# Instructions that read freshly loaded decay rows, queued behind the latest traced eviction

## The chip, the cores and the metric

The kernel runs on one core of one Trainium2 chip. The time is that of one execution on the device in microseconds (us); a run is repeated and the median is given. TensorE (PE in the profile) multiplies into PSUM, VectorE (DVE), ScalarE (ACT) and GpSimd (POOL) work elementwise, and SyncE (SP) issues transfers. Each engine takes its instructions in the order of its own queue, and an instruction that waits holds up those behind it.

## What is computed

One layer of a streaming encoder over 576 frames (a prompt of 512 and a sample of 64) of width 1024, in float32:

```python
def layer(x, lp, st):
    h = x + 0.5 * swiglu(rmsnorm(x, lp['norm_ffn1']), lp['w_ffn1_in'], lp['w_ffn1_out'])
    mix, new_st = mixer(rmsnorm(h, lp['norm_mix']), lp, st)
    h = h + mix
    h = h + 0.5 * swiglu(rmsnorm(h, lp['norm_ffn2']), lp['w_ffn2_in'], lp['w_ffn2_out'])
    return h, new_st
```

The mixer projects its input once and feeds three branches: band attention of 8 heads, an SSD scan (Mamba-2) of 16 heads in 4 groups, and an mLSTM scan of 4 heads. Both scans weigh products of a chunk with decays, exponentials of differences of running sums. For the SSD scan:

```python
cum = jnp.cumsum(dtc * a, axis=1)
seg = cum[:, :, None] - cum[:, None, :]
lmat = jnp.exp(jnp.where(causal, seg, -jnp.inf))
cb = jnp.einsum('btgn,bsgn->btsg', cc, bc)
w = cb[..., None] * lmat * dtc[:, None]
y = jnp.einsum('btsgr,bsgrp->btgrp', w, xc)
y = y + jnp.exp(cum)[..., None] * jnp.einsum('btgn,bgrpn->btgrp', cc, h)
last = cum[:, -1]
wd = jnp.exp(last[:, None] - cum) * dtc
h = jnp.exp(last)[..., None, None] * h + jnp.einsum('bsgr,bsgn,bsgrp->bgrpn', wd, bc, xc)
```

The mLSTM scan has the same shape, with a running maximum as stabiliser.

## The kernel before

Activations lie with features on the 128 partitions and the 576 frames along the free axis. A float32 product is made of three products of rounded parts (high by high, high by low, low by high): ACT rounds a weight piece (line 334) and DVE takes the rest (line 335). Most products go through seven block products in place of eight on 2x2 blocks of the matrices: POOL and accumulating transfers add the weight blocks (lines 548 and 560), and each product (line 704, twelve matmuls) lands in a PSUM bank.

In the mixer the projections are a stream of such products, seven to a pair of output tiles (`pairs`). Each product's bank is emptied by one instruction: `tmp` (line 621, ACT, into `uv`), or `emit` (line 628 on ACT, line 630 on DVE). The evictions have a raised priority. The next product but a few in the same bank can start only when its bank has been emptied.

Between the products the branches' own work is traced as jobs. `product` calls `tick`, which lets the job at the head of a list trace its next piece, up to a `yield n` that asks for n ticks of pause. The jobs are attention (`attn`), mLSTM heads (`ml`) and SSD groups (`ssd`), in the order a0 a1 m0 s0 a2 a3 s1 m1 s2 m2 s3 m3.

The decay rows are computed once (`gates`), written to DRAM (`scr`) and loaded back spread over the partitions: `decays` loads a pair of rows (line 188, ACT's queue) into one of three pairs of slots of `R1` (R in the profile), one pair ahead of its use; `ssd` also loads a pair into `ec` (line 1359, ACT's queue). What reads them:

- `ml`: `qt` = q times a row (line 1158, POOL); D from the row and a column of the small table TM (line 1162, DVE, five pieces), then Exp; `wc` (line 1180, ACT, five columns).
- `ssd`, for each of two halves of a group: `wd` (lines 1333 and 1334, DVE), `el` (1336 and 1337, ACT), Exp of `wd` (1338), which scales x into `xw` (1342, ACT); Relu of each of two rows in five pieces (1349, ACT), then Exp (1351 and 1352), then POOL's product with cb (1353 and 1354), which TensorE multiplies (1392); and Exp of `ec` (1383, ACT). TensorE uses `xw` for the states (1367). Each group starts with six Silu instructions (1287 and 1290).

The order on each engine is a planner's: it runs through the traced instructions with its own estimate of times and takes, on each engine, what is ready, the earliest traced first but for raised priorities. An instruction can thus stand on its engine far ahead of others that were traced before it, if its inputs are ready by that estimate. `issue_after(i)` adds an order of issue behind `i` for what a block traces on `i`'s engine, with no wait for its end; `keep_in_program_order(i)` puts `i` behind the instruction traced last ahead of it on its engine.

Of the kernel before, what the change touches and what calls it, by code (L numbers as in the profile page):

```python
# [28 lines left out]
AF = mybir.ActivationFunctionType  # L29
ALU = mybir.AluOpType  # L30
# [5 lines left out]
CH = [(0, 128), (128, 128), (256, 128), (384, 128), (512, 64)]  # L36
# [49 lines left out]
class Hybrid:  # L86
    def __init__(self, ctx, tc, I, O):
        self.tc, self.nc, self.I, self.O = tc, tc.nc, I, O
        self.op = None
        self.stay = {}  # L90
        self.plan = []
        self.splan = []
        self.ahead = {}
        self.steps = None
        self.b_i, self.b_n, self.fetched = 0, 0, deque()
        self.behind = 0
        self.jobs, self.gap, self.side = deque(), 0, iter(())
# [12 lines left out]
        self.gs = [self.dram.tile([128, T], F32, name=f"gs{i}") for i in range(24)]  # L110
        self.scr = self.dram.tile([24, T], F32, name="scr_rows")
# [496 lines left out]
    def pairs(self, seq):  # L608

        nc = self.nc
        order = ((0, self.T_X1), (0, self.T_A11), (1, self.T_A22), (0, self.T_X4), (0, self.T_X3), (1, self.T_X2),
                 (0, self.T_A21))
        H = (slice(0, FH), slice(FH, T))

        def tmp(ps, scale):
            o = self.gp.tile([128, FH], F32, name="uv", tag="uv", bufs=4)
            with self.tc.high_priority(offset=EVAC):  # L620
                nc.scalar.activation(o, ps, AF.Copy, scale=scale)  # L621
            return o

        def emit(ps, scale, other=None, op=None):
            def go(dst, a=0, b=FH, func=None):
                with self.tc.high_priority(offset=EVAC):
                    if other is None:
                        nc.scalar.activation(dst, ps[:, a:b], func or AF.Copy, scale=scale)  # L628
                        return
                    nc.vector.scalar_tensor_tensor(dst, ps[:, a:b], scale, other[:, a:b], op0=ALU.mult, op1=op)  # L630
                if func:
                    nc.scalar.activation(dst, dst, func)
            return go

        def pair(tiles, done):
            ((name, c1), s1, put1), ((_, c2), s2, put2) = tiles
            o = {}

            def on(t, ps):
                if t == self.T_X1:  # L640
                    o["v"] = tmp(ps, s1)
                elif t == self.T_X4:
                    o["m6"] = tmp(ps, s2)
                elif t == self.T_A11:
                    put1(1, H[1], emit(ps, s1, o["v"], ALU.add))
                elif t == self.T_X3:
                    o["u"] = tmp(ps, s2)
                elif t == self.T_A21:
                    put2(1, H[1], emit(ps, s2, o["u"], ALU.subtract))
                elif t == self.T_A22:  # L650
                    put2(0, H[0], emit(ps, -s2, o["m6"], ALU.add))
                else:
                    put1(0, H[0], emit(ps, s1))
                    if done:
                        done()
            return (name, 0, c1, c2), self.T, on

        self.stream([pair(*p) for p in seq], order, lambda n: {self.T_X1: n % 2, self.T_X4: 2, self.T_A11: 2})

    def tick(self):
        next(self.side, None)
# [479 lines left out]
    def ml(self, h, t):  # L1144
        nc = self.nc
        q, k, v, o = t["q"], t["k"], t["v"], t["o"]
        i = self.b()
        nmB, eiB = self.R1[:, i, :], self.R1[:, i + 1, :]
# [6 lines left out]
        self.tok_major(v, v1)  # L1155
        yield 1
        qt = self.t("t")
        nc.gpsimd.tensor_tensor(qt, q, eiB, op=ALU.mult)

        D = self.P()  # L1160
        for c, (a, n) in enumerate(CH):
            nc.vector.tensor_scalar(D[:n, a:a + n], nmB[:n, a:a + n], self.TM[:n, c, 64 + h:65 + h], 0.0,
                                    op0=ALU.add, op1=ALU.min)
        nc.scalar.activation(D[:, :512], D[:, :512], AF.Exp)
        nc.scalar.activation(D[:64, 512:], D[:64, 512:], AF.Exp)
        dv = D[:, :512].rearrange("p (c t) -> p c t", t=128)
# [2 lines left out]
        s = self.ps("s")  # L1169
# [6 lines left out]
        self.empties(nc.vector.tensor_tensor(D[:64, 512:], s2[:64, :64], D[:64, 512:], op=ALU.mult))  # L1176

        wc = self.unit([128, 8], "wc", 2)
        for c, (a, n) in enumerate(CH):
            nc.scalar.activation(wc[:n, c:c + 1], self.TM[:n, c, 64 + h:65 + h], AF.Exp, bias=nmB[:n, a + n - 1:a + n])  # L1180
        yield 2
        nums = [self.ps("v"), self.ps("x")]
        where = [(0, 0), (0, 129), (0, 258), (1, 0), (1, 129)]
# [1 line left out]
        for c, (a, n) in enumerate(CH):  # L1185
# [22 lines left out]
        r = self.unit([128, 8], "r", 2)  # L1208
# [3 lines left out]
        for c, (a, n) in enumerate(CH):  # L1212
            b, o0 = where[c]
# [3 lines left out]
        for c, (a, n) in enumerate(CH):  # L1217
            b, o0 = where[c]
# [63 lines left out]
    def ssd(self, g, t):  # L1282
        nc = self.nc
# [3 lines left out]
        last = nc.scalar.activation(self.R1[:, 0, :], self.R1[:, 0, :], AF.Silu)  # L1287
# [8 lines left out]
        ps = self.ps("s")  # L1296
# [5 lines left out]
        ps = self.ps("s")  # L1302
# [6 lines left out]
        for j in range(2):  # L1309
            x = t[f"x{j}"]  # L1310
            d0 = 4 * g + 2 * j
            i = self.b()
            free += [i, i + 1]
            cum = self.R1[:, i, :], self.R1[:, i + 1, :]
# [4 lines left out]
            ps = self.ps("x")  # L1319
# [4 lines left out]
            ps = self.ps("x")  # L1324
# [3 lines left out]
            wd = self.unit([128, 5, 2], "wd", 2)  # L1328
            el = self.unit([128, 5, 2], "el", 2)
            nc.gpsimd.memset(wd[:, 4, :], 0.0)  # L1330
            for r in range(2):
                last = cum[r][:, 127:512:128]
                nc.vector.tensor_tensor(wd[:, 0:4, r], last, self.TM[:, 0:4, 32 + d0 + r], op=ALU.subtract)
                nc.vector.tensor_tensor(wd[:64, 4:5, r], cum[r][:64, 575:576], self.TM[:64, 4:5, 32 + d0 + r],
                                        op=ALU.subtract)
                nc.scalar.activation(el[:, 0:4, r], last, AF.Exp)
                nc.scalar.activation(el[:, 4:5, r], cum[r][:, 575:576], AF.Exp)
            nc.scalar.activation(wd, wd, AF.Exp)
            for c, (a, n) in enumerate(CH):
                for r in range(2):  # L1340
                    hs = slice(r * 64, (r + 1) * 64)
# [3 lines left out]
            for r in range(2):  # L1345
                e = cum[r]
                tc_ = 32 + d0 + r
                for c, (a, n) in enumerate(CH):
                    nc.scalar.activation(e[:n, a:a + n], e[:n, a:a + n], AF.Relu, scale=-1.0,
                                         bias=self.TM[:n, c, tc_:tc_ + 1])  # L1350
                nc.scalar.activation(e[:, :512], e[:, :512], AF.Exp, scale=-1.0)
                nc.scalar.activation(e[:64, 512:], e[:64, 512:], AF.Exp, scale=-1.0)
# [10 lines left out]
            for c, (a, n) in enumerate(CH):  # L1363
                if c == 4:
                    states[4] = s0
                ps = self.ps("s")
                nc.tensor.matmul(ps[:, :128], bt[:n, c, :], xw[:n, c, :], start=True, stop=True)
                new = st()
                if c == 0:
                    i = nc.scalar.copy(new, ps[:, :128])  # L1370
                else:
                    h = states[c]
                    for r in range(2):
                        hs = slice(r * 64, (r + 1) * 64)
                        i = nc.vector.scalar_tensor_tensor(new[:, hs], h[:, hs], el[:, c, r:r + 1], ps[:, hs],
                                                           op0=ALU.mult, op1=ALU.add)
# [6 lines left out]
            nc.scalar.activation(ec, ec, AF.Exp)  # L1383
# [368 lines left out]
```

## Time and profile before

| | |
|---|---|
| median of 3 runs | 1923.6 us (1921.49 to 1924.52) |
| profiled execution | 1917.74 us |
| its span, first to last instruction | 1916.0 us |
| mean granted TensorE clock | 0.992 |
| transfers of rows into R (line 188) | 12 of 576 KB, median 5.8 us to landing |
| transfers into `ec` (line 1359) | 16 of 144 KB, median 5.4 us to landing |

The profile is of one execution. Busy time is the time in which an engine ran at least one instruction; TensorE's is modelled, as its matmuls are pipelined. Where a row ends in brackets, they hold how long the engine stood idle before that instruction and what it waited for last. A granted clock of 1.00 is TensorE's full speed.

### The profile page before, as it was taken

The page shows a single profiled execution, that of the slowest core. Times are in us where ns is not written, and L with a number is a line of the kernel's source. Part 1 is how long each engine was busy: PE and PEld are TensorE (multiplying, and loading weights), DVE is VectorE, ACT ScalarE, POOL GpSimd, SP SyncE. Part 2 cuts the span into 40 slices and gives each one's busy share as a digit, 9 for nine tenths or more (in the row PEclk, how much of TensorE's full clock was granted, in tenths as well). Part 3 has the DMA queues.
Part 4 walks back from the last instruction along what each step waited for, and adds up shares of the span by engine and source line. Part 5 has one row for each costly group of instructions (what it writes and reads, how often), then busy time and mean ns, then how long its engine had stood idle before and what let it go on. Part 6 is the DMA issues. An engine that isn't in the chain of part 4 may idle for free. (4 is left out here: it accounts for less than half of the span.)

```text
span 1916.0 us, 37655 instructions
## 1 busy us (share of the span) xinstructions
PE 1862.7 (97%) x13901; PEld 1811.8 (95%) x13901; DVE 1534.0 (80%) x2715; ACT 1090.5 (57%) x2502; POOL 673.1 (35%) x645
## 2 busy tenths in 40 slices
PE   9899999999999989999999999999999999999998
PEld 9899999999999769988989889999999999999998
DVE  7998998998768858678787866745898998889865
ACT  6564654654534786777766666334565564554544
POOL 3433333343302225324445343530334333333311
PEclk9999999999999999999999999999999999999999
DMA  7366666666643445764667665642546666666631
GB/s 224 103 154 173 162 156 165 154 176 170 176 133 99 139 140 142 211 174 116 178 165 186 169 159 168 215 171 80 124 111 168 169 154 169 165 155 168 154 99 56
DMA packets 129439, 294.69 MB, mean 154 GB/s; under 512 B 14288, under 2 KB 26192, under 8 KB 129256
## 3 DMA queue, kind: packets, MB, share of 16 engines
q1 hardware_dynamic: 99368, 203.42, 32.6%
q0 software_dynamic: 20272, 74.20, 21.0%
q10 hardware_dynamic: 9616, 14.69, 2.7%
q8 instruction: 109, 1.79, 0.4%
q14 instruction: 74, 0.61, 0.1%
HBM read 272.87 MB, written 19.38 MB: 153 GB/s over the span
## 5 line engine op out<-in xcount | busy, mean ns | idle before, releaser
L704 PE MATMUL acc<-TH,ph 128*128 128x288 f32 x3220 | 965.0, 300 | 28.3 <-ACT uv L621 9.0
L704 PE MATMUL acc<-TL,ph 128*128 128x288 f32 x3220 | 954.7, 297 | 1.3 <-DVE TL L335 1.2
L704 PE MATMUL acc<-TH,pl 128*128 128x288 f32 x3220 | 950.6, 296 | 0.3 <-DVE pl L335 0.3
L704 PEld LDWEIGHTS acc<-TH,ph 128*128 128x128 f32 x3220 | 605.8, 188 | 46.7 <-ACT uv L621 12.2
L704 PEld LDWEIGHTS acc<-TL,ph 128*128 128x128 f32 x3220 | 607.3, 189 | 3.8 <-DVE TL L335 2.4
L704 PEld LDWEIGHTS acc<-TH,pl 128*128 128x128 f32 x3220 | 607.6, 189 | 3.0 <-issue 2.1
L335 DVE TENSOR_TENSOR pl<-wr,ph 128x512 fp32r<-128x512 f32 x471 | 443.7, 948 | 72.9 <-ACT ph L334 61.2
L334 ACT CAST ph<-wr 128x512 fp32r<-128x512 f32 x471 | 287.5, 618 | 262.1 <-PE acc L704 136.6
L335 DVE TENSOR_TENSOR pl<-wx,ph 128x512 fp32r<-128x512 f32 x390 | 325.9, 839 | 35.1 <-ACT ph L334 28.8
L334 ACT CAST ph<-wx 128x512 fp32r<-128x512 f32 x390 | 237.0, 619 | 183.8 <-POOL wx L560 98.8
L560 POOL TENSOR_TENSOR wx<-wx,wr 128x512 f32<-128x512 f32 x160 | 246.3, 1540 | 184.9 <-DVE pl L335 150.2
L548 POOL DMA_DIRECT2D wx<-in_sblk x115 | 101.5, 916 | 482.5 <-DVE pl L335 167.6
L279 PE MATMUL acc<-YH,ph 128*128 128x256 f32 (+1 forms) x768 | 227.1, 298 | 2.4 <-ACT g L628 2.0
L279 PE MATMUL acc<-YL,ph 128*128 128x256 f32 (+1 forms) x768 | 227.2, 297 | 0.6 <-DVE YL L392 0.6
L279 PE MATMUL acc<-YH,pl 128*128 128x256 f32 (+1 forms) x768 | 226.9, 296 | 0.0
L279 PEld LDWEIGHTS acc<-YH,ph 128*128 128x128 f32 x768 | 145.2, 190 | 3.4 <-ACT g L628 2.2
L279 PEld LDWEIGHTS acc<-YL,ph 128*128 128x128 f32 x768 | 145.3, 189 | 1.1 <-DVE YL L392 1.0
L279 PEld LDWEIGHTS acc<-YH,pl 128*128 128x128 f32 x768 | 145.2, 189 | 0.0
L560 POOL TENSOR_TENSOR wy<-wx,wr 128x512 f32<-128x512 f32 x35 | 55.7, 1591 | 128.3 <-DVE pl L335 90.2
L743 DVE SCALAR_TENSOR_TENSOR R<-acc,R 128x288 f32<-128x288 f32 x168 | 75.7, 451 | 19.3 <-PE acc L704 18.8
L334 ACT CAST TH<-g 128x288 fp32r<-128x288 f32 x120 | 51.4, 433 | 53.4 <-POOL g L729 32.3
L335 DVE TENSOR_TENSOR pl<-wy,ph 128x512 fp32r<-128x512 f32 x70 | 62.0, 886 | 19.7 <-ACT ph L334 19.5
(330 smaller groups left out, 2351.7 us busy)
## 6 DMA issues: line engine op xcount, KB each, us to landing
wr<-in_sblk SPq DMA_DIRECT2D x345, 256.0 KB, 3.8
wx<-in_sblk POOLq DMA_DIRECT2D x119, 512.0 KB, 6.7
wx<-in_sblk SPq DMA_DIRECT2D x111, 512.0 KB, 3.8
wr<-in_wblk SPq DMA_DIRECT2D x126, 256.0 KB, 3.1
R<-scr_rows ACTq DMA_DIRECT2D x12, 576.0 KB, 5.8
gs<-g SPq DMA_DIRECT2D x20, 288.0 KB, 2.9
g<-gs POOLq DMA_DIRECT2D x20, 288.0 KB, 3.8
y<-ys POOLq DMA_DIRECT2D x12, 288.0 KB, 4.8
```

The costliest lines, as they stand in the source:

```text
L279: last = nc.tensor.matmul(ps[:, :n], wt[:, wsl], xx[:, k0 + k, a:a + n], start=(k == 0 and i == 0), stop=(k == nk - 1 and i == 2))
L334: self.cast = self.nc.scalar.copy(hi, src).ins
L335: self.nc.vector.tensor_tensor(lo, src, hi.bitcast(F32), op=ALU.subtract)
L548: nc.gpsimd.dma_start(x12, src[:, 1:3, :], accum_op=ALU.add)
L560: add = lambda o, one, two: self.nc.gpsimd.tensor_tensor(o, one, two, op=ALU.add)
L704: self.nc.tensor.matmul(ps, wt[:, wsl], xx[:, kk, :], start=(start and kk == 0 and i == 0), stop=(kk == 3 and i == 2), skip_group_check=True)
L743: self.nc.vector.scalar_tensor_tensor(o, ps, scale, o, op0=ALU.mult, op1=ALU.add)
```

## The change

The kernel remembers the last traced eviction on ACT and on DVE. A block `behind_products` queues what is traced in it on either engine behind that engine's remembered eviction. The instructions that read freshly loaded rows on ACT and DVE are put in such blocks, and `qt` on POOL is kept behind the instruction traced ahead of it.

```diff
+        self.evicted = {}
...
-                nc.scalar.activation(o, ps, AF.Copy, scale=scale)
+                self.evicted["ACT"] = nc.scalar.activation(o, ps, AF.Copy, scale=scale).ins
...
-                        nc.scalar.activation(dst, ps[:, a:b], func or AF.Copy, scale=scale)
+                        self.evicted["ACT"] = nc.scalar.activation(dst, ps[:, a:b], func or AF.Copy, scale=scale).ins
                         return
-                    nc.vector.scalar_tensor_tensor(dst, ps[:, a:b], scale, other[:, a:b], op0=ALU.mult, op1=op)
+                    self.evicted["DVE"] = nc.vector.scalar_tensor_tensor(dst, ps[:, a:b], scale, other[:, a:b],
+                                                                         op0=ALU.mult, op1=op).ins
...
+    @contextmanager
+    def behind_products(self):
+
+        with ExitStack() as s:
+            for i in self.evicted.values():
+                s.enter_context(self.tc.issue_after(i))
+            yield
...
-        nc.gpsimd.tensor_tensor(qt, q, eiB, op=ALU.mult)
+        self.tc.keep_in_program_order(nc.gpsimd.tensor_tensor(qt, q, eiB, op=ALU.mult))
...
+        with self.behind_products():
+            for c, (a, n) in enumerate(CH):
+                nc.vector.tensor_scalar(D[:n, a:a + n], nmB[:n, a:a + n], self.TM[:n, c, 64 + h:65 + h], 0.0,
+                                        op0=ALU.add, op1=ALU.min)
...
+        with self.behind_products():
+            for c, (a, n) in enumerate(CH):
+                nc.scalar.activation(wc[:n, c:c + 1], self.TM[:n, c, 64 + h:65 + h], AF.Exp, bias=nmB[:n, a + n - 1:a + n])
...
+            with self.behind_products():
+                for r in range(2):
+                    last = cum[r][:, 127:512:128]
+                    nc.vector.tensor_tensor(wd[:, 0:4, r], last, self.TM[:, 0:4, 32 + d0 + r], op=ALU.subtract)
+                    nc.vector.tensor_tensor(wd[:64, 4:5, r], cum[r][:64, 575:576], self.TM[:64, 4:5, 32 + d0 + r],
+                                            op=ALU.subtract)
+                    nc.scalar.activation(el[:, 0:4, r], last, AF.Exp)
+                    nc.scalar.activation(el[:, 4:5, r], cum[r][:, 575:576], AF.Exp)
+                nc.scalar.activation(wd, wd, AF.Exp)
...
+                with self.behind_products():
+                    for c, (a, n) in enumerate(CH):
+                        nc.scalar.activation(e[:n, a:a + n], e[:n, a:a + n], AF.Relu, scale=-1.0,
+                                             bias=self.TM[:n, c, tc_:tc_ + 1])
...
+            with self.behind_products():
+                nc.scalar.activation(ec, ec, AF.Exp)
```

More of the change, by code (lines that the diff above doesn't have):

```diff
@@ L1157, in ml @@
         qt = self.t("t")
-        nc.gpsimd.tensor_tensor(qt, q, eiB, op=ALU.mult)
+        self.tc.keep_in_program_order(nc.gpsimd.tensor_tensor(qt, q, eiB, op=ALU.mult))
         D = self.P()
-        for c, (a, n) in enumerate(CH):
-            nc.vector.tensor_scalar(D[:n, a:a + n], nmB[:n, a:a + n], self.TM[:n, c, 64 + h:65 + h], 0.0,
-                                    op0=ALU.add, op1=ALU.min)
+        with self.behind_products():
+            for c, (a, n) in enumerate(CH):
+                nc.vector.tensor_scalar(D[:n, a:a + n], nmB[:n, a:a + n], self.TM[:n, c, 64 + h:65 + h], 0.0,
+                                        op0=ALU.add, op1=ALU.min)
         nc.scalar.activation(D[:, :512], D[:, :512], AF.Exp)
@@ L1178, in ml @@
         wc = self.unit([128, 8], "wc", 2)
-        for c, (a, n) in enumerate(CH):
-            nc.scalar.activation(wc[:n, c:c + 1], self.TM[:n, c, 64 + h:65 + h], AF.Exp, bias=nmB[:n, a + n - 1:a + n])
+        with self.behind_products():
+            for c, (a, n) in enumerate(CH):
+                nc.scalar.activation(wc[:n, c:c + 1], self.TM[:n, c, 64 + h:65 + h], AF.Exp, bias=nmB[:n, a + n - 1:a + n])
         yield 2
@@ L1330, in ssd @@
             nc.gpsimd.memset(wd[:, 4, :], 0.0)
[L1331 to L1338, printed above, removed]
+            with self.behind_products():
[7 more added lines that the diff above has]
+                nc.scalar.activation(wd, wd, AF.Exp)
             for c, (a, n) in enumerate(CH):
@@ L1347, in ssd @@
                 tc_ = 32 + d0 + r
-                for c, (a, n) in enumerate(CH):
-                    nc.scalar.activation(e[:n, a:a + n], e[:n, a:a + n], AF.Relu, scale=-1.0,
-                                         bias=self.TM[:n, c, tc_:tc_ + 1])
+                with self.behind_products():
+                    for c, (a, n) in enumerate(CH):
+                        nc.scalar.activation(e[:n, a:a + n], e[:n, a:a + n], AF.Relu, scale=-1.0,
+                                             bias=self.TM[:n, c, tc_:tc_ + 1])
                 nc.scalar.activation(e[:, :512], e[:, :512], AF.Exp, scale=-1.0)
@@ L1382, in ssd @@
                     yield 1
-            nc.scalar.activation(ec, ec, AF.Exp)
+            with self.behind_products():
+                nc.scalar.activation(ec, ec, AF.Exp)
             D = self.cst[:, C_D + 2 * g + j:C_D + 2 * g + j + 1]
```

## The prediction

> **What bounds the kernel now.** I read the page's first lines first, then busy time and granted clock by stretch, then who TensorE waits for, and then the order of time around each wait.
>
> ```profile
> span 1916.0 us, 37655 instructions
> ...
> PE 1862.7 (97%) x13901; PEld 1811.8 (95%) x13901; DVE 1534.0 (80%) x2715; ACT 1090.5 (57%) x2502; POOL 673.1 (35%) x645
> ```
>
> The span is TensorE's: 1862.7 of 1916.0 us. Nothing in the change touches a product's own work, so it can give back only TensorE's idle time (53.3 us in all) and time at a lowered clock. The next view gives, for each stretch, length, busy time of PE, PEld, DVE, ACT and POOL, granted clock, and DMA.
>
> ```profile
> core 0: us, PE busy (x) PEld busy (x) DVE busy (x) ACT busy (x) POOL busy (x), PEclk, DMA share, GB/s
> 0.00:600.00 600.00, 591.07 (x4369) 585.92 (x4370) 519.29 (x845) 320.02 (x658) 199.46 (x179) 0.99 0.60 160
> 600.00:1200.00 600.00, 566.42 (x4263) 524.56 (x4262) 451.30 (x933) 420.69 (x1137) 234.40 (x244) 0.99 0.58 160
> 1200.00:1916.00 716.00, 705.16 (x5273) 701.34 (x5271) 563.43 (x938) 349.74 (x707) 239.25 (x223) 1.00 0.53 144
> 676.00:700.00 24.00, 16.48 (x129) 11.63 (x127) 10.83 (x34) 21.68 (x71) 3.70 (x5) 0.86 0.60 169
> ...
> 768.00:774.00 6.00, 5.87 (x33) 5.87 (x34) 4.81 (x8) 2.59 (x7) 2.57 (x2) 0.72 0.26 67
> ```
>
> The stretch from 600 to 1200 us, the mixer's three branches, holds 600 - 566.4 = 33.6 us of TensorE's idle time, and all the instructions of the diff lie in it. From 676 to 700 us alone TensorE idles 24 - 16.48 = 7.5 us at a clock of 0.86, while ACT is busy 21.68 of 24 us.
>
> ```profile
> PE acc L704 <- ACT uv L621: 9.0, 10, 2.3
> PE acc L704 <- ACT g L628: 5.7, 4, 2.0
> ```
>
> These are TensorE's two longest waits (us in total, times, longest): both are for ACT emptying a product's bank. One case in order of time, with [idle before <- releaser] at the end of a row:
>
> ```profile
> 976.30 1.04 ACT L1180 ACTIVATE wc<-TM,R 128x1 f32<-128x1 f32 x5 [2.68 <-DMA R<-scr_rows]
> ...
> 977.59 0.39 ACT L621 ACTIVATE uv<-acc 128x288 f32<-128x288 f32 x1
> ```
>
> ```profile
> 978.03 0.40 PE L704 MATMUL acc<-TH,ph 128*128 128x288 f32 x1 [1.55 <-ACT uv L621]
> ```
>
> ACT stands 2.68 us at `wc`, whose decay row has not landed; the eviction behind it in the queue could have run, comes late, and TensorE loses 1.55 us. No other work of TensorE covers this. That is the bound the change aims at.
>
> **Why these instructions stand there.** They need only rows and the small table TM, so the planner put them far ahead of their head.
>
> ```profile
> L1349 ACT ACTIVATE R<-R,TM x80: 332/394/432, 677.2 to 1055.5; 128x128 f32<-128x128 f32 x64, 64x64 f32<-64x64 f32 x16
> ```
>
> ```profile
> L1342 ACT ACTIVATE t<-t,wd x80: 331/333/352, 759.2 to 1134.7; 128x64 f32<-128x64 f32 x64, 64x64 f32<-64x64 f32 x16
> ```
>
> Lines 1349 and 1342 belong to the same head pair and are traced in the same step, but the first decay activation runs at 677.2 us and the first scaling of `xw` at 759.2: 82 us apart; for the last ones 1134.7 - 1055.5 = 79 us. With an order edge behind the eviction traced last ahead, each must come down to about where `xw` is. So the edges bind, nearly all of them.
>
> **The change part by part.** Moved: in each of 8 SSD halves 4 DVE subtractions, 4 `el`, 1 `wd`, 10 Relu and 1 `ec` on ACT; in each of 4 mLSTM heads 5 DVE instructions and 5 `wc`. That is 52 on DVE and 148 on ACT; none is added or removed, and none of them issues a DMA. The row loads themselves (line 188, on ACT's queue) get no edge. The big Exp of lines 1351 and 1352 follow their Relus by data. An edge is an order of issue only, on one engine, so no new semaphore wait is added.
>
> *Part 1: loads in front of an eviction.* The other cases, ACT and then TensorE (the first waits not for a load but for DVE's `wd`, early work of the next group too):
>
> ```profile
> 765.76 1.28 ACT L1338 ACT_TABLE_LOAD   x1 [1.67 <-DVE wd L1334]
> ```
>
> ```profile
> 929.60 0.68 ACT L1383 ACTIVATE ec<-ec 128x576 f32<-128x576 f32 x1 [2.05 <-DMA ec<-scr_rows]
> ```
>
> ```profile
> 1033.52 0.68 ACT L1383 ACTIVATE ec<-ec 128x576 f32<-128x576 f32 x1 [1.53 <-DMA ec<-scr_rows]
> ```
>
> ```profile
> 1074.88 0.85 ACT L1180 ACTIVATE wc<-TM,R 128x1 f32<-128x1 f32 x4 [4.45 <-DMA R<-scr_rows]
> ```
>
> ```profile
> 1137.68 1.28 ACT L1383 ACT_TABLE_LOAD   x1 [2.23 <-DMA ec<-scr_rows]
> ```
>
> ```profile
> 768.13 0.40 PE L704 MATMUL acc<-TH,ph 128*128 128x288 f32 x1 [2.31 <-ACT uv L621]
> ```
>
> ```profile
> 931.15 0.40 PE L704 MATMUL acc<-TH,ph 128*128 128x288 f32 x1 [1.99 <-ACT g L628]
> ```
>
> ```profile
> 1035.07 0.40 PE L704 MATMUL acc<-TH,ph 128*128 128x288 f32 x1 [1.02 <-ACT g L628]
> ```
>
> ```profile
> 1077.31 0.40 PE L704 MATMUL acc<-TH,ph 128*128 128x288 f32 x1 [1.04 <-ACT P L628]
> ```
>
> ```profile
> 1140.53 0.40 PE L704 MATMUL acc<-TH,ph 128*128 128x288 f32 x1 [1.22 <-ACT g L628]
> ```
>
> TensorE loses 1.55 + 2.31 + 1.99 + 1.02 + 1.04 + 1.22 = 9.1 us. The 2.31 us cost more: in the stretch 768 to 774 the clock is 0.72, so 6 x 0.28 = 1.7 us are lost again. Together 10.8 us. After the change a row of the head that is 80 us away can't stand in front of an eviction, and `ec`, loaded two ticks ahead, stands behind one. What is late next: the cast of a weight piece or the next eviction, about 0.4 to 0.6 us each. Bounds 0 (the wait moves to the next eviction) and 10.8; the rows show the loads landing at most 4.45 us late and the instructions move by tens of us, so I take 9.
>
> The Trainium skill ("TensorE: Matmul & The Clock Gate", HAM oscillation) says the clock falls only after idle gaps of more than about 3.4 us; by it the stall of 2.31 us would cost itself alone and part 1 would be 9.1 us at most. The trace here disagrees: the 0.72 stands right behind a gap of 2.31 us, and the row decides.
>
> *Part 2: the early work itself.* ACT's groups from 676 to 695 us (busy us, mean ns):
>
> ```profile
> L1349 ACT ACTIVATE R<-R,TM 128x128 f32<-128x128 f32 (+1 forms) x20 | 6.7, 397 | 0.0
> L1351 ACT ACTIVATE R<-R 128x512 f32<-128x512 f32 x4 | 2.6, 643 | 0.0
> ...
> L1180 ACT ACTIVATE wc<-TM,R 128x1 f32<-128x1 f32 (+1 forms) x5 | 1.3, 309 | 0.0
> ...
> L1352 ACT ACTIVATE R<-R 64x64 f32<-64x64 f32 x4 | 1.1, 274 | 0.0
> ```
>
> ```profile
> 685.86 0.40 PE L704 MATMUL acc<-TH,ph 128*128 128x288 f32 x1 [1.47 <-ACT g L628]
> ...
> 690.09 0.33 PE L1044 MATMUL ps_x<-ident,P 128*128 128x128 f32 x1 [1.40 <-ACT P L1035]
> ...
> 693.15 0.48 PE L1044 MATMUL ps_x<-ident,P 128*128 128x128 f32 x1 [2.01 <-ACT P L1035]
> ```
>
> 6.7 + 2.6 + 1.3 + 1.1 = 11.7 of these 19 us of ACT are decays for heads that come 30 to 80 us later, and in between TensorE stands behind ACT's evictions and softmax. The stretch 676 to 700 loses 7.5 us of idle time and 24 x 0.14 = 3.4 us by the clock: 10.9 us, the bound from above; from below 0. ACT is not alone there:
>
> ```profile
> 698.41 0.58 ACT L1073 ACTIVATE P<-ps_s,sm 128x384 f32<-128x384 f32 x1 [2.00 <-DVE sm L1072]
> ```
>
> After the last early decay, ACT itself waits 2.00 us for DVE: the attention job's own chain remains. I take six tenths, the early decays' share of ACT (11.7 of 19): 6.5 us.
>
> *Part 3: what it costs where it arrives.* Each group now does its own 11 to 12 us of decays instead of the next group's. ACT has room:
>
> ```profile
> 890.00:945.00 55.00, 50.94 (x396) 47.99 (x396) 36.98 (x69) 38.17 (x100) 27.07 (x30) 1.00 0.61 163
> ```
>
> 38.17 of 55 us are busy around the second group, and that already holds decays of the third. But they now come right behind the group's Silu block, where ACT is behind already:
>
> ```profile
> 747.56 1.28 ACT L1287 ACT_TABLE_LOAD   x1
> 748.85 0.69 ACT L1287 ACTIVATE R<-R 128x576 f32<-128x576 f32 x1
> ```
>
> ```profile
> 897.85 0.40 PE L704 MATMUL acc<-TH,ph 128*128 128x288 f32 x1 [1.12 <-ACT uv L621]
> ```
>
> ```profile
> L1336 ACT ACTIVATE el<-R x16: 192/203/221, 674.0 to 1049.5; 128x4 f32<-128x4 f32 x16
> ```
>
> The table load back to Exp (1.28) and four `el` and `wd` (5 x 0.2 = 1.0) join that backlog: at most 2.3 us a group if all of it stands ahead of an eviction, 9.1 us in four; below, nothing, since the edges put each behind the eviction of its own step, and even a gain of 3 us is possible, because the table loads at 765.76 and 1137.68 now stand in front of evictions as well. I take 1.1 a group, as the 1.12 above: 4.5 us. In the Trainium skill ("ScalarE: Activation LUTs", What ACT_TABLE_LOAD costs) a switch is put at about 2.66 us with its drain, which would make this term some 10 us; in this trace the Silu starts 1.29 us after its load does, so 1.28 stands.
>
> ```profile
> DVE wd L1333 <- DMA R<-scr_rows: 11.6, 6, 4.0
> ```
>
> DVE's 52 instructions I cost at nothing either way: DVE stands 11.6 us for rows now, and none of the waits of part 1 is TensorE's for DVE. On POOL, `qt` (line 1158) is pinned behind the instruction traced ahead of it:
>
> ```profile
> L1158 POOL TENSOR_TENSOR t<-g,R x4: 1426/1542/1711, 726.2 to 1150.0; 128x576 f32<-128x576 f32 x4
> ```
>
> It runs at the end of each head's preparation with POOL 35% busy; queued behind it are the weight sums (line 560) and the accumulating loads (line 548), which SP's loads then wait for only through the ring. I cost it at nothing; if that cover is gone it is 1.5 us a head, 6 us.
>
> **Sum:** 9 + 6.5 - 4.5 = 11 us gained. The profiled execution took 1917.7 us beside its span of 1916.0, and would take 1906.7. The median of before is 1923.6, 5.9 us above that execution; the same 11 us off the median give **1912.6 us**.
>
> **The rivals.**
> *A, slower: just-in-time decays.* The place is the SSD half: `wd`, `xw` and the Relu, Exp and POOL product must now all be made between the transposes of x and the products of lines 1367 and 1392, where before only `xw` was. If ACT lags there, TensorE stands in its queue at 1367 or 1392. Price: a stall as long as the longest above, 2.31 us, in each of 8 halves, 18.5 us, and a clock window of 1.7 in each of four groups, 6.8: 25.3 against gains of 15.5, so +10, 1933. It decides from 2 us a half on (15.5 / 8). For it: the chain is longer by some 5 us of ACT ((11.7 - 1.3) / 2). Against it: the planner can put products between, and ACT is 69% busy (38.17 / 55).
>
> *B, no change: the gain is taken back.* The attention job is bound by its own ping-pong of DVE and ACT (the 2.00 above), part 2 gives 1 us instead of 6.5, part 1 gives 9 less 3 for evictions that still queue, and part 3 takes 4.5: 1 + 6 - 4.5 = 2.5 us gained, 1921.
>
> *C, the change does nothing,* because the eviction remembered is an old one that is ahead anyway: 1923.6. The 82 us between lines 1349 and 1342 speak against it.
>
> **How the numbers follow.** Forecast 0.62, A 0.16, B 0.19, C 0.03. About 0.2% (3.8 us) is what a measurement of this kernel can tell from no change: faster is below 1919.8. The forecast's cases and a fifth of B lie there, 0.66; the rest of B, with C, 0.18; slower 0.16. Range: below, parts 1 and 2 whole and part 3 at nothing, 10.8 + 10.9 = 21.7 us, is 1902; above, B and the near end of A, to 1927.
>
> **What would show it.** Right: line 1349 from about 755 to 1135 us instead of 677 to 1055; no wait of DVE or ACT for R over 1 us; ACT under 16 us in 676 to 700 and the clock there at 0.95 or more; the six stalls of part 1 gone. Wrong: TensorE waits at lines 1367 or 1392, or the rows `uv` and `g` keep their 14.7 us (9.0 + 5.7) with other things in front; more table loads than eight in the mixer; POOL's sums late behind `qt`.

## The result, and the profile after

| | before | after |
|---|---|---|
| median | 1923.06 us (6 runs, 1921.49 to 1924.52) | 1908.11 us (6 runs, 1904.71 to 1909.50) |
| profiled execution | 1917.74 us | 1908.66 us |
| its span | 1916.0 us | 1906.9 us |

The ratio is 0.992, 95% interval 0.9908 to 0.9933: 15.0 us between the medians, 9.1 us between the two profiled executions. The rest, 5.9 us, is where the profiled executions lie among their kernels' runs: that of before is 5.3 us under its median (and below all six runs), that of after 0.6 us over its own.

Line numbers are now those of the changed kernel, one higher than before up to the evictions and ten to fifteen higher behind them. `el` is now 1349 and 1350, `xw` 1355, the Relu 1363, the Exp 1365 and 1366, the states' product 1381, the decay product 1407, `wc` 1192, `ec` 1398; the evictions are 622 (`uv`), 629 (ACT) and 631 (DVE), the product is 714. "Changed kernel" is the kernel after; "rows" are the decay rows of R and `ec`. The page's first lines after:

```profile
span 1906.9 us, 37698 instructions
...
PE 1860.4 (98%) x13901; PEld 1811.6 (95%) x13901; DVE 1527.5 (80%) x2715; ACT 1091.0 (57%) x2502; POOL 676.7 (35%) x645
```

Busy time by stretch after (columns as in the prediction: length, PE, PEld, DVE, ACT, POOL, granted clock, DMA):

```profile
600.00:1200.00 600.00, 573.25 (x4332) 534.43 (x4331) 452.14 (x946) 425.62 (x1145) 238.97 (x249) 0.99 0.58 163
...
676.00:700.00 24.00, 20.52 (x150) 15.91 (x149) 10.75 (x31) 14.58 (x43) 3.70 (x5) 0.86 0.50 142
768.00:774.00 6.00, 6.00 (x56) 5.51 (x55) 4.72 (x8) 3.77 (x12) 4.04 (x5) 1.00 0.82 194
```

TensorE's own work is nearly the same (1860.4 us busy against 1862.7). Its idle time from 600 to 1200 us fell from 33.6 to 26.75 us; from 676 to 700 it fell from 7.5 to 3.5, and ACT there from 21.68 to 14.58. That is 6.8 us of the 9.1. The other 2.3 us are TensorE's busy time, for the same 13901 matmuls: the lowered clock behind the stall at 768 is gone, which gives 1.7; the remaining 0.6 us is not explained.

Where the Relus and the first `el` stand now, by source line (count, min/median/max ns, first and last start):

```profile
L1363 ACT ACTIVATE R<-R,TM x80: 332/388/407, 753.1 to 1123.9; 128x128 f32<-128x128 f32 x64, 64x64 f32<-64x64 f32 x16
```

```profile
L1349 ACT ACTIVATE el<-R x16: 191/208/212, 752.6 to 1112.3; 128x4 f32<-128x4 f32 x16
L1349 ACT ACT_TABLE_LOAD  x4: 1283/1283/1283, 751.3 to 1097.5; - x4
```

The Relus came down from 677 to 753 us. No wait of ACT or DVE for a row is left between 600 and 1200 us (before: 17.1 us on ACT, 12.1 on DVE). What TensorE waits for there now:

```profile
PE acc L714 <- ACT uv L622: 8.2, 9, 1.5
PE acc L714 <- DVE g L631: 3.5, 4, 1.2
PE acc L714 <- ACT g L629: 3.0, 3, 1.1
```

The evictions are still what TensorE waits for, but nothing in front of them waits for a transfer any more; they stand behind other work. One such place in order of time, ACT and then TensorE:

```profile
895.07 1.27 ACT L1363 ACTIVATE R<-R,TM 128x128 f32<-128x128 f32 x4
...
896.58 0.62 ACT L1365 ACTIVATE R<-R 128x512 f32<-128x512 f32 x1
...
898.33 1.78 ACT L1355 ACTIVATE t<-t,wd 128x64 f32<-128x64 f32 x7
...
901.19 0.40 ACT L629 ACTIVATE g<-acc 128x288 f32<-128x288 f32 x1
```

```profile
901.64 0.40 PE L714 MATMUL acc<-TH,ph 128*128 128x288 f32 x1 [1.08 <-ACT g L629]
```

The first row's five Relus and its Exp run ahead of the ten `xw` copies, and the eviction behind all of them comes late: TensorE waits 1.08 us. This place matters for what follows.

### The profile page after: what moved, and what is told of

It reads as the page before. It is cut to its first block, busy times and chain, and to the rows that moved or that the text cites. A ratio compares the mean times of both kernels' runs of the same rounds, so it can differ in the third digit from the quotient of the medians.

```text
span 1906.9 us, 37698 instructions
## 1 busy us (share of the span) xinstructions
PE 1860.4 (98%) x13901; PEld 1811.6 (95%) x13901; DVE 1527.5 (80%) x2715; ACT 1091.0 (57%) x2502; POOL 676.7 (35%) x645
## 5 line engine op out<-in xcount | busy, mean ns | idle before, releaser
L336 DVE TENSOR_TENSOR pl<-wx,ph 128x512 fp32r<-128x512 f32 x390 | 316.8, 816 | 30.5 <-ACT ph L335 24.0
L561 POOL TENSOR_TENSOR wy<-wx,wr 128x512 f32<-128x512 f32 x35 | 59.7, 1705 | 131.4 <-DVE pl L336 97.2
```

The source lines that it names most:

```text
L336: self.nc.vector.tensor_tensor(lo, src, hi.bitcast(F32), op=ALU.subtract)
L561: add = lambda o, one, two: self.nc.gpsimd.tensor_tensor(o, one, two, op=ALU.add)
```

## The experiments

All times below are medians, and each ratio is against runs of the kernel before, timed beside it on the same chip. The ratios are those on record; some differ by 0.001 from the quotient of the two medians (for "rows apart" below, 1904.71 over 1922.23 is 0.9909, on record 0.9901), so a difference of 0.001 between two kernels says nothing. The theory to begin with: the gain is the waits for rows that no longer stand in front of evictions. Its rivals: one group of edges does it all, or any order of ACT's work that keeps a block of it out of the way of an eviction does.

### One group of edges alone

The kernels leave edges out in this form (shown for the Relus; the mLSTM group is `D` and `wc`). The pin on `qt` is left out as well where only `ec` or only the Relus keep their edge; it stays with `D` and `wc`. The group of `wd` and `el` was neither run alone nor left out alone.

```
-                with self.behind_products():
+                with nullcontext():
                     for c, (a, n) in enumerate(CH):
                         nc.scalar.activation(e[:n, a:a + n], e[:n, a:a + n], AF.Relu, scale=-1.0,
```

Only `ec` keeps its edge:

> Only the Exp of ec (one instruction in each SSD half, 8 in all) is queued behind the evictions; wc, D, wd, el, Relu and qt are as before the change. My theory (TensorE loses what ACT's wait for a row costs the eviction behind it): the stalls of 1.99, 1.02 and 1.22 us behind ec go, the others stay: 3 to 5 us faster than before. Rival (the planner's order as a whole shifts and the gain is an accident of it): any value, with the three stalls replaced by others. Rival (the waits move to the next instruction that reads a row): no change.

Only the Relus keep theirs:

> Only the Relu of the decays is queued behind the evictions (with it, by data, the big Exp). My theory: the early work leaves the stretch of the second attention job (676 to 700 us), worth the 4 us that the changed kernel gained there; the waits for wc, ec and wd stay: 3 to 6 us faster. Rival (only the waits for loads matter): within 1.5 us of before.

Only `D` and `wc` keep theirs:

> Only the mLSTM heads' part: D and wc behind the evictions, qt pinned. My theory: the stalls of 1.55 and 1.04 us behind wc go, and 1.3 us of early wc leave the attention job: 2 to 4 us faster. Rival (accident of the order): any value.

Measured: `ec` alone 1920.63 us, ratio 1.0001 (0.999 to 1.0012); Relus alone 1924.59, 1.0019 (1.0002 to 1.0037); `D` and `wc` alone 1923.82, 1.0018 (1.0 to 1.0036). None of the three gains, where each was expected to be 2 to 6 us faster. Waits of the kernel with the Relus alone, ACT and then DVE (us in total, times, longest):

```profile
ACT wc L1192 <- DMA R<-scr_rows: 15.8, 4, 4.5
ACT el L1349 <- DMA R<-scr_rows: 8.8, 3, 4.5
```

```profile
DVE wd L1346 <- DMA R<-scr_rows: 19.0, 7, 5.5
```

Before, `wc` waited 9.8 and `wd` 11.6 us. The room that the Relus leave is filled with the early readers that are still free, and these then wait for their rows: the waits grow. In the kernel with `ec` alone, DVE stands 7.50 us at `wd`, and a cast on DVE that TensorE needs is late:

```profile
949.66 0.17 DVE L1346 TENSOR_TENSOR wd<-R,TM 128x4 f32<-128x4 f32 x1 [7.50 <-DMA R<-scr_rows]
```

```profile
950.69 0.40 PE L714 MATMUL acc<-TH,pl 128*128 128x288 f32 x1 [2.27 <-DVE pl L336]
```

### All groups but one

> Everything of the change but the edges on Relu. If the parts simply add: faster by the whole gain less what relu_alone gains, 9 to 12 us. My theory: Relu is then the first reader of a fresh row on ACT and stands in front of evictions with the wait that wd and el had, so part of it comes back: 4 to 8 us faster than before, with waits of ACT for R at the Relu's line.

> The SSD part of the change whole (wd, el, Relu, ec), the mLSTM heads' part as before the change (D, wc and qt free). The single parts gained nothing, so the new theory: what is left free moves into the room on ACT, ahead of its row, and waits. By it wc waits 2.5 to 4.5 us for R three or four times in front of evictions: ratio to before 0.994 to 0.998. Rival (mLSTM's part is worth nothing, as it gained nothing alone): 0.992, as the changed kernel. Rival (only the whole order counts, each gap undoes all of it): 0.999 or more.

> The change without the edge on the Exp of ec (8 instructions of 0.68 us). By the theory ec moves ahead into a place where its row has not landed: waits of ACT of 1 to 5 us, ratio to before 0.994 to 0.998. Rival (ec is too small to matter, as it gained nothing alone): 0.992.

Measured: all but the Relus' edge 1920.01 us, 0.999 (0.9979 to 1.0001); all but `D` and `wc` 1916.06, 0.9967 (0.9953 to 0.998); all but `ec` 1906.70, 0.9909 (0.9888 to 0.993).

**Without `D` and `wc`** (and without the pin on `qt`) somewhat under half of the gain stays, and the profile shows the loss as the theory has it: `wc` stands 4.76 us at a row, the eviction comes behind it, and TensorE is 3.45 us late.

```profile
1079.14 1.04 ACT L1192 ACTIVATE wc<-TM,R 128x1 f32<-128x1 f32 x5 [4.76 <-DMA R<-scr_rows]
...
1080.94 0.40 ACT L629 ACTIVATE P<-acc 128x288 f32<-128x288 f32 x1
```

```profile
1081.39 0.61 PE L714 MATMUL acc<-TH,ph 128*128 128x288 f32 x1 [3.45 <-ACT P L629]
```

**Without `ec`'s edge** nothing is lost in all, although its waits are back; the expected 0.994 to 0.998 was missed:

```profile
ACT ec L1398 <- DMA ec<-scr_rows: 14.0, 6, 5.0
```

ACT waits 14.0 us, and TensorE idles 600 - 572.21 = 27.8 us from 600 to 1200, much as in the changed kernel (26.75). That is a balance, not a proof that no wait costs. The longest of the six does reach TensorE: behind it ACT's cast of a weight piece is late, then DVE's part of it, then DVE's eviction.

```profile
797.08 0.68 ACT L1398 ACTIVATE ec<-ec 128x576 f32<-128x576 f32 x1 [5.00 <-DMA ec<-scr_rows]
```

```profile
799.68 0.40 PE L714 MATMUL acc<-TH,ph 128*128 128x288 f32 x1 [1.95 <-DVE g L631]
```

Behind the waits of 2.78, 1.30, 0.45 and 0.43 us TensorE has no stall that the changed kernel hasn't, but for two of 0.3 us; 5 us behind that of 4.00 us, at 1042.62, it has one of 1.06 us, which may be its doing. In return TensorE idles 1.35 us from 676 to 700 where the changed kernel idles 3.5; why is not shown. So a wait for a row need not cost anything; the place decides.

**Without the Relus' edge** comes the result that broke the theory, by which it would be 4 to 8 us faster, with ACT waiting for rows at the Relus. No wait for a row is left on ACT or DVE, as in the changed kernel, and yet the time is about that of before: TensorE idles 600 - 567.21 = 32.8 us. Of the 11.8 us between its span (1918.7 us) and the changed kernel's, 7.6 are TensorE's idle time (54.1 against 46.5 us over the whole span) and 4.2 its busy time, for the same matmuls at a lower clock: from 600 to 1200 us the clock was at half for 27.3 us, against 13.7. Its waits in that kernel, and one place on ACT and TensorE:

```profile
PE acc L714 <- ACT uv L622: 6.5, 8, 1.1
PE acc L714 <- ACT g L629: 6.1, 3, 2.3
PE ps_s L1381 <- ACT t L1355: 2.4, 1, 2.4
```

```profile
901.29 1.27 ACT L1363 ACTIVATE R<-R,TM 128x128 f32<-128x128 f32 x4
...
902.57 1.74 ACT L1363 ACTIVATE R<-R,TM 64x64 f32<-64x64 f32 x6
904.21 0.61 ACT L1365 ACTIVATE R<-R 128x512 f32<-128x512 f32 x1
...
905.96 1.78 ACT L1355 ACTIVATE t<-t,wd 128x64 f32<-128x64 f32 x7
...
908.30 0.40 ACT L629 ACTIVATE g<-acc 128x288 f32<-128x288 f32 x1
```

```profile
908.75 0.54 PE L714 MATMUL acc<-TH,ph 128*128 128x288 f32 x1 [1.90 <-ACT g L629]
```

It is the place shown above of the changed kernel. There five Relus (four at 895.07 and one more) run ahead of the copies and the eviction, here all ten (four and six), 1.90 us of stall for 1.08. The edges on `wd` and `el` hold the Relus down by data, since the Relu overwrites the row that `el` reads: the rows have landed, but the block of work is in front.

### Moving work on ACT with all edges kept

Two edits keep every edge and spread ACT's blocks. One sets the two rows' Relu and Exp a tick apart, behind `xw`:

```
             for r in range(2):
+                yield 1
                 e = cum[r]
...
                 if r == 0:
-                    yield 1
                     ec = self.unit([128, T], "ec", 1)
...
-            yield 2
+            yield 1
```

> The changed kernel with the two rows' Relu, Exp and product of each SSD half traced one tick each after the scaling of xw (ticks 1 and 2 in place of 0 and 1; the sum of the ticks is the same). If blocks of ACT in front of evictions are what TensorE loses now, the stalls of 1.08, 1.09, 0.85 and 1.52 us behind Relu, Exp and xw shrink: 2 to 5 us faster than the changed kernel, ratio to before 0.989 to 0.991. Rival (the products of the decays come too late and TensorE waits at line 1408): 0.993 or more.

The other sets three of six Silus a tick later:

```
-            for v in (Bf, Cf, t["x0"], t["x1"], self.R1[:, 1, :]):
+            for v in (Bf, Cf):
                 nc.scalar.activation(v, v, AF.Silu)
-        yield 2
+        yield 1
+        with self.behind_products():
+            for v in (t["x0"], t["x1"], self.R1[:, 1, :]):
+                nc.scalar.activation(v, v, AF.Silu)
+        yield 1
```

> The changed kernel, and of the six Silu that start an SSD group (4.8 us of ACT in one piece with the table load) three are traced one tick later, behind the latest eviction. If blocks of ACT in front of evictions are what TensorE loses now, the three stalls of 1.12 us behind the Silu block and those of 0.3 us at the transposes shrink: 2 to 4 us faster than the changed kernel, ratio to before 0.990 to 0.991. Rival (the planner puts the work back together, or x comes late): 0.992 or more.

Measured: rows apart 1904.71 us, 0.9901 (0.9879 to 0.9922); Silus split 1906.20, 0.9912 (0.9892 to 0.9932). With the rows apart, ACT at the same place, and the stretch (the Relu is line 1364 there):

```profile
898.73 2.50 ACT L1355 ACTIVATE t<-t,wd 128x64 f32<-128x64 f32 x10
...
902.69 0.40 ACT L629 ACTIVATE g<-acc 128x288 f32<-128x288 f32 x1
...
905.02 2.92 ACT L1364 ACTIVATE R<-R,TM 128x128 f32<-128x128 f32 x10
```

```profile
600.00:1200.00 600.00, 579.78 (x4374) 541.40 (x4374) 453.60 (x955) 427.48 (x1147) 242.49 (x252) 0.99 0.59 165
```

All ten Relus now come behind the `xw` copies and the evictions; the stalls at the three places like 901.64 are gone, and TensorE idles 20.2 us for 26.75. Note that the ten are still one block: it isn't cut up, it stands elsewhere. The fourth stall named in the expectation, 1.52 us at 760.34, did not shrink but grew to 1.76. No Relu stands in front of that eviction now, but the ten `xw` copies, which wait for DVE and have no edge:

```profile
759.25 2.50 ACT L1355 ACTIVATE t<-t,wd 128x64 f32<-128x64 f32 x10 [0.82 <-DVE t L1334]
```

```profile
762.61 0.40 PE L714 MATMUL acc<-TH,ph 128*128 128x288 f32 x1 [1.76 <-ACT uv L622]
```

The split Silus did half of what was expected. The three stalls of 1.12 us are gone, but those at the transposes, which were to shrink, grew from 0.3 to 2.1 us: the three late Silus had no order against the early two and ran ahead of them, and the transposes of B waited:

```profile
883.62 0.66 PE L1007 MATMUL ps_x<-ident,g 128*128 128x128 f32 x4 [2.06 <-ACT g L1302]
```

So the next kernel ties the late three behind the first Silu as well, with the rows apart:

```
+        with self.tc.issue_after(last.ins), self.behind_products():
+            for v in (t["x0"], t["x1"], self.R1[:, 1, :]):
```

> The changed kernel with the rows' Relu and Exp a tick apart, and with three of the six Silus (x0, x1, z1) a tick later, behind the first Silu of the group and behind the products. Theory (what is left of TensorE's stalls in the mixer are ScalarE's blocks in front of evictions, and the 2.1 us stalls of the first split came from the three late Silus running ahead of those of B and C): the stalls at 885 to 890, 988 to 994 and 1090 to 1097 us fall from 2.1 to under 0.5, TensorE's idle time from 600 to 1200 us to 15 to 19 us, the clock loses no more than 7 us there, and the ratio is 0.985 to 0.989, 1895 to 1902 us. Rival (a later Silu brings more table loads, since the row's Exps come between: 12 in the mixer for 8 at 1.28 us each): the ratio is 0.990 to 0.993, no better than the rows apart alone.

Measured: 1903.23 us (1902.32 to 1904.35), 0.9909 (0.9894 to 0.9925). The 2.06 us stalls are gone, but the one behind the Silu block stayed at 1.12 us in two of the three groups; TensorE idles 19.5 us from 600 to 1200, so the expected 0.985 to 0.989 was missed, and the time can't be told from that with the rows apart alone. It is the lowest median of all kernels run. Both are below the changed kernel's 1908.11, but were not timed beside it, and their intervals overlap with its own.

### Is it the Relu's place, and which?

Three runs separate what the Relu's edge does. With the rows apart but no edge on the Relus:

> The changed kernel with the two rows' Relu and Exp set one tick apart behind the xw copies, and no edge on the Relus (the other edges stay). Theory (the Relu's edge is worth what it is because it breaks up the block of ten Relus, three or four Exps and the copies in front of an eviction, not because it keeps a wait for a row away): the tick apart does the same breaking, so TensorE has no stall over 1.2 us behind a block of line 1363, no wait for a row stands on ScalarE, and the ratio is 0.990 to 0.994, 1904 to 1911 us. Rival (only the edge to the product itself does it; the planner draws the untied Relus together again whatever ticks they are written in): the stalls of 1.9 to 2.3 us at the second rows are back, as in the kernel with all edges but the Relu's, and the ratio is 0.997 to 1.001.

With the rows apart and no edges at all:

> The kernel before with the two rows' Relu and Exp set one tick apart, and no edge at all. Theory (the edges are needed, since the planner fills room on ScalarE and VectorE with early readers that then wait for their rows): waits for rows stay at 10 us or more on ScalarE and on VectorE, and the ratio is 0.996 to 1.001, 1914 to 1925 us. Rival (most of the gain is the order of ScalarE's work in ticks, and the edges bring it only by moving the Relus): the ratio is 0.990 to 0.994.

And with the Relus tied behind the last `xw` copy in place of the evictions:

```
-                    nc.scalar.activation(xw[:n, c, hs], xd[:n, c, hs], AF.Copy, scale=wd[:n, c, r:r + 1])
+                    xl = nc.scalar.activation(xw[:n, c, hs], xd[:n, c, hs], AF.Copy, scale=wd[:n, c, r:r + 1])
...
-                with self.behind_products():
+                with self.tc.issue_after(xl.ins):
                     for c, (a, n) in enumerate(CH):
```

> The changed kernel with the Relus of line 1363 tied behind the last xw copy of line 1355 in place of the products' evictions; all other edges stay. Theory (what costs 13 us without the Relu's edge is only that the ten Relus and the Exps of line 1365 run ahead of the xw copies, on which the states' product and the eviction behind it wait): with the Relus behind xw, TensorE's stalls of 1.9 to 2.3 us at the second rows are gone or under 1.1 us, no wait for a row stands on ScalarE in the mixer, TensorE idles 20 to 27 us from 600 to 1200 us, and the ratio is 0.989 to 0.993, 1901 to 1909 us. Rival (the Relus must stand behind the evictions themselves, since a block of Relus and Exps right behind xw delays the next g and uv evictions as much): stalls of 1.5 us or more behind line 1363 or 1365 remain, TensorE idles 30 us or more there, and the ratio is 0.996 to 1.001.

Measured: rows apart without the Relu's edge 1918.25 us, 0.999 (0.9981 to 1.0); rows apart without edges 1920.41, 0.9992 (0.9981 to 1.0004); Relus behind `xw` 1918.58, 0.998 (0.997 to 0.999). My theory missed the first and the third, and its rivals were right in both. In the first the planner drew the ten Relus together ahead of the copies again, a tick apart in the code or not:

```profile
899.64 1.26 ACT L1364 ACTIVATE R<-R,TM 128x128 f32<-128x128 f32 x4
...
900.91 1.74 ACT L1364 ACTIVATE R<-R,TM 64x64 f32<-64x64 f32 x6
```

With the Relus behind `xw` the copies are early, as with the rows apart, but the Relus follow at once, and the eviction comes behind them:

```profile
897.18 2.50 ACT L1355 ACTIVATE t<-t,wd 128x64 f32<-128x64 f32 x10
899.59 2.38 ACT L1363 ACTIVATE R<-R,TM 128x128 f32<-128x128 f32 x8
...
903.95 0.40 ACT L629 ACTIVATE g<-acc 128x288 f32<-128x288 f32 x1
```

```profile
904.40 0.40 PE L714 MATMUL acc<-TH,ph 128*128 128x288 f32 x1 [1.96 <-ACT g L629]
```

The stall is 1.96 us, as long as with the Relus in front of the copies (1.90). So it is not that the copies were late: it is whatever ACT does in front of the eviction, as the 1.76 us behind the copies alone showed too. What the edge must name is the eviction.

### What the runs say together

| kernel | ratio | rows waited for, ACT / DVE us | TensorE idle 600 to 1200, us | span of the profiled execution, us |
|---|---|---|---|---|
| before | 1 | 17.1 / 12.1 | 33.6 | 1916.0 |
| changed | 0.992 | 0 / 0 | 26.75 | 1906.9 |
| `ec` alone | 1.0001 | 12.0 / 18.0 | 36.4 | 1919.6 |
| Relus alone | 1.0019 | 26.9 / 22.8 | 40.4 | 1924.6 |
| `D`, `wc` alone | 1.0018 | 12.9 / 18.4 | 39.9 | 1925.9 |
| all but Relu | 0.999 | 0 / 0 | 32.8 | 1918.7 |
| rows apart, no edge on Relu | 0.999 | 0 / 0 | 33.2 | 1916.3 |
| Relu behind `xw` | 0.998 | 0.7 / 0 | 33.1 | 1917.8 |
| rows apart, no edges | 0.9992 | 21.8 / 15.4 | 38.1 | 1920.0 |
| all but `D`, `wc` | 0.9967 | 15.1 / 4.2 | 35.8 | 1916.4 |
| all but `ec` | 0.9909 | 14.0 / 0 | 27.8 | 1904.3 |
| rows apart | 0.9901 | 0 / 0 | 20.2 | 1903.3 |

The three kernels with next to no row waits and little or no gain (0.998 to 0.999) show that taking the waits away is not enough. The kernel with 14.0 us of row waits and the whole gain shows that taking all of them away is not needed either. What the fast ones have in common, by the rows shown, is that few early readers, waiting or working, stand on ACT in front of an eviction that TensorE is about to need. The idle column is of one execution and goes with the span beside it, not with the ratio: all but `D` and `wc` idles more than before (35.8 against 33.6 us) and has the better ratio, but its execution is 2.0 us over its median and that of before 5.3 us under, and their spans are nearly the same.

## Why the prediction was right, and where it was not

The forecast of 1912.6 us was 4.5 us above the 1908.11 measured, inside its range, and faster was the likeliest sign. The bound it named is the right one: evictions on ACT that are late, and TensorE's idle time and clock behind them. The sizes of its parts fit less well, as the steps show, in the two profiled executions:

- **That the edges bind** (rival C out): right. Line 1349 of before, now 1363, first starts at 753.1 and last at 1123.9 us, forecast about 755 to 1135.
- **Part 1, rows in front of evictions, 9 us:** right for the rows it named, and a little low. The six stalls are gone, 9.1 us, and with them the clock window at 768 (0.72 before, 1.00 after): 10.8.
- **Part 2, early work in the attention stretch, 6.5 us:** too high. Idle time fell by 4.0 us. ACT dropped under 16 us as forecast (14.58), but the clock stayed at 0.86 where 0.95 was expected. The attention's own chain still stalls TensorE, once by 1.89 us, and the slow clock follows that:

```profile
688.72 0.44 PE L1054 MATMUL ps_x<-ident,P 128*128 128x128 f32 x2 [1.89 <-ACT P L1045]
```

```profile
690.00:696.00 6.00, 4.84 (x26) 4.17 (x25) 2.54 (x8) 3.46 (x12) 0.00 (x0) 0.54 0.00 0
```

- **Part 3, what it costs where it arrives, 4.5 us:** too low, and put at the wrong work. Idle time fell by 6.8 us, of which parts 1 and 2 are 9.1 + 4.0; so 6.3 us came in anew, net. The forecast looked for it behind the Silu block and the table load. The stall behind the Silu block is 1.12 us, as it was, and the table load stands just behind the `uv` eviction. The new cost stands behind the Relu, Exp and `xw` block: 1.08, 1.09 and 0.85 us at 901.64, 1005.68 and 1108.16, and 1.52 at 760.34, 4.5 in all. Five other new stalls, 0.99, 1.24 and 0.90 us behind DVE's eviction of `g` and twice 0.89 behind `uv`, have no instruction of the diff just ahead of them; others of before are gone in return (1.26 us at 1089.30), so that the net is 6.3.
- **The sum:** 10.8 + 4.0 - 6.3 = 8.5 against 11 forecast; the span shows 9.1. That the medians differ by 15.0 is the 5.9 us by which the two profiled executions stand differently to their medians; had that gap been the same for both, the kernel would have come out near 1914. So the forecast was about 2 us too high a gain by the executions and 4 us too low by the medians, with parts that missed by +1.8, -2.5 and -1.8 us: that the total came so near is in part luck.
- **Rival A** (TensorE waits at the products 1381 and 1407 for decays made just in time): not in the changed kernel, where line 1381 waits 0.3 us once. Its mechanism is real: without the Relu's edge TensorE waited 2.4 us at line 1381 for `xw`, as the waits above show, and 0.8 us at line 1407 for the decays. **Rival B** (evictions still queue, with other things in front) describes part of what is left: `uv` and `g` of ACT went from 14.7 us to 11.2, not to nothing.
- **`qt` on POOL, nothing:** no loss shows. It has no run of its own, so this isn't shown.

The reasoning that the runs corrected is the one under part 1, that a load in front of an eviction is what costs. It named real stalls, and it counted all edges as one. The runs show that they don't add: three of the four groups alone made the kernel no faster (ratios 1.0001 to 1.0019), and leaving out the Relus' edge alone, which guards against no wait, loses nearly all. The planner takes whatever reader is still free and puts it into the room ahead, so the gain comes when what is left free no longer reaches the front of an eviction. That the filling is the planner's is read from the order of the traces; no run shows the estimates by which it chose.

Open: why the runs of the kernel before mostly lie above its profiled execution. It lies inside the spread of all of them, 1913.59 to 1926.36 us in the longest series (31 runs). Kernels with many row waits spread more widely over ten runs (from 6.7 us for `ec` alone to 11.9 for the Relus alone) than those with next to none (5.1 to 5.9). That fits transfers landing sooner or later from one execution to the next, but only one execution of each was traced. Open too is what the edges on `wd` and `el` are worth by themselves, and the pin on `qt`.

## What to carry to other kernels

When a planner places work ahead because an engine has room, look at what ends up directly in front of the evictions that TensorE waits for, and tie exactly that behind the eviction; an order among the other instructions (`xw` before Relu, a tick apart in the code) did not do it here. Edges of this kind don't add up one by one, so take one away from the whole set rather than trying each alone: here the three groups tried singly gave nothing, and the one that hid no wait at all was worth most of the 15 us. A wait for a transfer on an engine's list is a cost only where the next thing behind it is due.

## What the runs showed of the hardware

TensorE's clock fell behind stalls of about 2 us, but not behind each. In every trace the lowered clock is a half clock that lasts 3.413 us or a whole multiple of it, and within one execution such stretches start whole multiples of 3.413 us apart (in that of before at 663.7, 691.1 and 769.6 us, 8 and 23 of them apart). So each execution has a fixed grid of windows of 3.413 us. Two stalls of 1.90 us in the kernel with all edges but the Relu's (at 908.75 and 1016.17), each with the window of the grid in which it ends, and the next one:

```profile
905.44:908.85 3.41, 1.51 (x12) 1.32 (x10) 1.11 (x2) 3.41 (x13) 1.18 (x3) 1.00 0.71 171
908.85:912.27 3.42, 3.42 (x15) 3.42 (x16) 2.60 (x5) 2.83 (x9) 2.98 (x3) 0.50 0.55 170
...
1014.67:1018.08 3.41, 1.87 (x12) 1.63 (x12) 1.45 (x2) 3.41 (x12) 1.78 (x4) 1.00 0.62 198
1018.08:1021.50 3.42, 3.33 (x32) 3.00 (x33) 3.42 (x7) 2.77 (x11) 3.34 (x3) 1.00 0.21 59
```

The first stall lies in one window, in which TensorE idles 3.41 - 1.51 = 1.90 us, and the next window runs at half clock. The second began in the window ahead, leaves 3.41 - 1.87 = 1.54 us of idle time in this one, and the clock stays at 1.00. The kernel with the Relus behind `xw` shows the same with a stall of 1.96 us (1.57 us in one window, then 1.00) and one of 2.02 us (all of it in one window, then 0.50). Of all windows at full clock in the fourteen traces, the first 20 and last 12 us left out, the 41 in which TensorE idled 1.9 us or more were each followed by half clock, none of the 5156 with less than 1.0 us was, and 31 of the 146 between were. So it is not the length of one stall that decides but the idle time in one window, and a halved window costs up to 1.7 us. TensorE's busy time is modelled, so these bounds are rough.

The Trainium skill ("TensorE: Matmul & The Clock Gate", What's actually happening) says that the activity is watched in a free-running window of about 3.4 us. The traces agree, with 3.413 us. Its section HAM oscillation gives as the rule that no idle gap be longer than about 3.4 us. Here the clock fell behind 1.90 us, as behind the 2.31 us of the prediction.
